# A row vector kept in two adjacent PSUM banks while a fused transformer kernel runs its front, with six banks in rotation

## The chip, the cores and the metric

One NeuronCore of a Trainium2 chip runs the whole program in one launch. The metric is device time in microseconds (us). Of the kernel before there are three runs, with a median of 1686.18 us (1681.76 to 1689.4), and one execution under the profiler.

## The reference, cut to what matters

The reference is a small model on one sequence of 256 tokens with a width of 1024, in fp32. Every block of its first part is modulated by a vector that comes from a condition `c`:

```python
def modulation(cs, w, b):
    m = cs @ w + b                      # cs: 1 x 1024, w: 1024 x 3072
    shift, scale, gate = jnp.split(m, 3, axis=-1)
    return shift[:, None, :], scale[:, None, :], gate[:, None, :]

cs = jax.nn.silu(c)
for i in range(DEPTH):                  # DEPTH = 2
    shift, scale, gate = modulation(cs, mod_mix_w[i], mod_mix_b[i])
    h = x * (1.0 + scale) + shift
    y = mla_mixer(h, ...) if i == 0 else s5_mixer(h, ...)
    x = layer_norm(ALPHA * x + (1.0 + gate) * y, ln_mix_g[i], ln_mix_b[i])
    shift, scale, gate = modulation(cs, mod_ffn_w[i], mod_ffn_b[i])
    h = x * (1.0 + scale) + shift
    y = sq_relu_mlp(h, mlp_w1[i], mlp_b1[i], mlp_w2[i], mlp_b2[i])
    x = layer_norm(ALPHA * x + (1.0 + gate) * y, ln_ffn_g[i], ln_ffn_b[i])
```

A second part of two layers follows: gated MLPs before and after a mixer, which is a recurrent block with a convolution and a gated linear recurrence in the first layer, and block attention with a bias in the second.

## The kernel before

All weights are streamed from device memory once, in blocks of 128 rows of 1024 columns (512 KB), in the order in which they are needed; `run` takes the next blocks of that list. A block of a matrix (`w`) is split into two fp32r tiles: ScalarE makes `wh`, a rounded copy (L464), and VectorE makes `wl`, the rest (L504; for some blocks GpSimd, L468). A matrix product is then three matmuls (xh by wh, xh by wl, xl by wh) that add up in a PSUM bank (L400). The activations are split the same way by `split` (L636 on ScalarE, L637 on VectorE).

A block of the modulation weights (`m`, each holds 128 outputs with 1024 inputs) doesn't go to TensorE. `mod_unit` multiplies it on VectorE with `cs`, the row silu(c) repeated on all 128 partitions (128 x 1024), and adds up along the row in the same instruction (L555). There are 96 such products; 40 of them run in the first 110 us, which the text calls the front. After each group of eight, L564 adds the bias.

The program is written in Python that calls the engines in program order (a manual schedule); each engine works off its own queue in that order, and waits between engines are put in by the tile framework from the tiles that instructions read and write.

PSUM is divided into eight bank tiles of 128 x 512. `self.free` is a queue of bank numbers: `bank()` takes the number at its front, `rel()` puts a bank that has been read at its end. So which bank a step gets follows from the order of takes and releases alone.

The order of the work, as far as the change and the prediction touch it:
- `setup` makes constants, and `cs` out of two banks (L1013 on ScalarE, L1014 on VectorE).
- `mla`: input projections; GpSimd computes the tables of the S5 mixer beside them (the rotations, L1421). Then `q_pair(0)` and `heads`, the loop over eight attention heads, with three further `q_pair`. A `q_pair` makes the queries of two heads on TensorE; VectorE turns part of them (L1227, L1228, L1229), and their sum is the operand of the scores. After the loop the output projection `mla_o` starts.
- From there on, for each block: `boundary` runs the last pass of a projection, the norm of its result, the transposes of the normed rows (L644, four into each of two banks), and `make_xt`, which applies scale and shift while it moves two banks to SBUF, one on ScalarE (L679), the other on VectorE (L677), in four pieces each; `xt_split` splits the result. Then `f_pass(0)` and `f_pass(1)` compute four hidden tiles for the two halves of the tokens into two banks each, and `f_evac` moves these out, one bank on ScalarE (L901), the other on VectorE (L902).

The pieces of `make_xt` are issued like this:

```python
for j in range(4):
    for g in range(2):
        if g:
            nc.vector.tensor_scalar(o, i, s[:, k:k + 1], sh[:, k:k + 1], op0=OP.mult, op1=OP.add)
        else:
            nc.scalar.activation(o, i, func=AF.Identity, scale=s[:, k:k + 1], bias=sh[:, k:k + 1])
```

Of the kernel before, what the change touches and what calls it, by code (L numbers as in the profile page):

```python
# [11 lines left out]
F32 = mybir.dt.float32  # L12
F32R = mybir.dt.float32r
I32 = mybir.dt.int32
AF = mybir.ActivationFunctionType
OP = mybir.AluOpType
# [296 lines left out]
class Model:  # L313
    def __init__(self, ctx, tc, ws, cols, rows, x, pos, inv, rel, sp, sbc, sgb, out):
        self.tc, self.nc = tc, tc.nc
        self.ws, self.rows_d, self.x_d, self.pos_d, self.inv_d = ws, rows, x, pos, inv
        self.cols_d, self.relb_d, self.sp_d, self.sbc_d, self.sgb_d, self.out_d = cols, rel, sp, sbc, sgb, out
        sb = self.sb = ctx.enter_context(tc.tile_pool(name="sb", bufs=1))
        ps = ctx.enter_context(tc.tile_pool(name="ps", bufs=1, space=bass.MemoryType.PSUM))
        dr = ctx.enter_context(tc.tile_pool(name="dr", bufs=1, space=bass.MemoryType.DRAM))  # L320
        T = lambda n, shape, dt=F32: sb.tile(shape, dt, name=n)
        self.raw = [T("raw%d" % i, [128, 1024]) for i in range(RAWN)]
        self.Hs, self.Ls = [None] * RING, [None] * RING
        self.pt = {u: sb.tile([128, 1024], F32, name="early%d" % j, tag="w%s%d" % ("hl"[j % 2], 4 + j // 2))
                   for j, u in enumerate(PUNITS)}
        self.lent = {4 + j: set(PUNITS[2 * j:2 * j + 2]) for j in range(5)}
        self.lent[9] = self.lent[10] = {"tables"}
        self.tabs = [[sb.tile([128, 1024], F32, name="rot%d%d" % (b, e), tag="w%s%d" % ("hl"[e], 9 + b)) for e in range(2)]
                     for b in range(2)]
        self.wide = [sb.tile([128, 2048], F32, name="wide%d" % i, tag="x%s" % "hl"[i]) for i in range(2)]  # L330
        self.rt, self.nop, self.opdone = [], 0, set()
        self.hidden(0)
        self.X = [T("x%d" % h, [128, 1024]) for h in range(2)]
        self.R = [T("r%d" % h, [128, 1024]) for h in range(2)]
        self.GATE, self.GR, self.BR, self.B2 = (T(n, [128, 1024]) for n in ("gate", "grow", "brow", "b2row"))
        self.Z = [T("z%d" % i, [128, 2048]) for i in range(3)]
        self.cols = T("cols", [128, NCOLS])
        self.ident = T("ident", [128, 128])
        self.mask = T("mask", [128, 128])
        self.identb, self.maskb = (T(n, [128, 128], mybir.dt.bfloat16) for n in ("identb", "maskb"))  # L340
        self.st = T("st", [128, 144])
        self.junk = T("junk", [128, 1024], mybir.dt.bfloat16)
        self.junka = T("junka", [128, 512], mybir.dt.bfloat16)
        self.mcol = [[T("mc%d%d" % (i, t), [128, 8]) for t in range(2)] for i in range(4)]
        self.scol, self.bcol = T("scol", [128, 8]), T("bcol", [128, 8])
        self.cs = T("cs", [128, 1024])
        self.msum, self.gcol = T("msum", [128, 8]), T("gcol", [128, 8])
        self.mhalf = T("mhalf", [128, 4])
        self.one = T("one", [128, 1])
        self.lri = T("lri", [128, 8], I32)  # L350
        self.banks = [ps.tile([128, 512], F32, name="bank%d" % i) for i in range(8)]
        self.free = deque(range(8))
        self.held = {}
        self.ops_d = dr.tile([12, 128, 1024], F32, name="ops_d")
        self.tab_d = dr.tile([4, 128, 1024], F32, name="tab_d")
        self.wt_d = dr.tile([2, 4, 2, 32, 64], F32, name="wt_d")
        self.stn = 0
        self.nproc = self.ntake = self.nw = 0
        self.pos_of, self.slot_owner = {}, [None] * RING
        self.slot_of, self.finished = {}, set()  # L360
        self.ndma = 0
        self.modfin, self.hold = None, False
        self.mods = set()
        self.pend = deque()
        self.lag, self.plo = False, deque()
        self.kept = {}
        self.xt32 = None
        self.bg = None
        self.bgt = 0.0
        self.fill = 0  # L370
# [8 lines left out]
    def bank(self):  # L379
        i = self.free.popleft()  # L380
        self.held[id(self.banks[i])] = i
        return self.banks[i]

    def rel(self, *bs):
        for b in bs:
            self.free.append(self.held.pop(id(b)))
# [158 lines left out]
    def mod_unit(self, u, raw):  # L545
        nc, tag, k = self.nc, u[1], u[2]
        i, third = int(tag[3]), int(tag[4])
        if k == 0 and third == 2:
            self.mod_finish()
        total = (self.gcol if tag == "mod01" else self.msum)[:, k:k + 1]  # L550
        if (tag, k) in POOLED:
            nc.gpsimd.tensor_tensor(raw, raw, self.cs, op=OP.mult)
            self.pend.append((raw, total))
        else:
            nc.vector.scalar_tensor_tensor(self.junk, raw, 1.0, self.cs, op0=OP.mult, op1=OP.mult, accum_out=total)  # L555
        if k == 7:
            self.settle(0)
        if tag == "mod01":
            if k == 7:
                self.mods.add(tag)  # L560
            return
        if k == 7:
            if third < 2:
                nc.vector.tensor_tensor(self.mcol[i][third], self.msum, self.col("modb%d" % i, 8 * third, 8), op=OP.add)  # L564
                self.mods.add(tag)
            else:
                nc.vector.tensor_tensor(self.gcol, self.msum, self.col("modb%d" % i, 16, 8), op=OP.add)
                nc.vector.tensor_scalar(self.gcol, self.gcol, 1.0, None, op0=OP.add)
                self.modfin = [tag, 3]
# [412 lines left out]
    def setup(self):  # L982
        nc = self.nc
        V, G = nc.vector, nc.gpsimd
        crow = self.GR[0:1, :]
        spt = self.wide[0][:, 768:768 + NSP]
        inv = self.wide[0][:, 864:896]
        posi = self.sb.tile([128, 2], I32, name="posi")
        nc.sync.dma_start(out=crow, in_=self.rows_d[ROWS["c"]:ROWS["c"] + 1, :])
        nc.sync.dma_start(out=spt, in_=self.sp_d)  # L990
        nc.sync.dma_start(out=posi, in_=self.pos_d)
        nc.sync.dma_start(out=inv, in_=self.inv_d)
        nc.sync.dma_start(out=self.cols, in_=self.cols_d)
        self._issue(2)
        for h in range(2):
            nc.sync.dma_start(out=self.X[h], in_=self.x_d[128 * h:128 * h + 128, :])
        self._issue(RAWN)
        half = self.Z[2][0:1, 0:128]
        V.memset(half, 0.5)
        V.memset(self.mhalf, -0.5)  # L1000
        V.memset(self.one, 1.0)
        jp = self.Z[0][:, 0:128]
        G.iota(jp, pattern=[[1, 128]], base=0, channel_multiplier=-1, allow_small_or_imprecise_dtypes=True)
        pi = self.sb.tile([128, 2], I32, name="pio")
        G.iota(pi[:, 0:1], pattern=[[0, 1]], base=0, channel_multiplier=1)
        V.tensor_scalar(self.ident, jp, 0.0, None, op0=OP.is_equal)
        V.tensor_scalar(self.mask, jp, 0.0, NEG, op0=OP.is_gt, op1=OP.mult)
        cb = [self.bank(), self.bank()]
        for n in range(2):
            self.mm(cb[n], half, crow[:, 512 * n:512 * n + 512], True, True)  # L1010
        for n in range(2):
            t = self.Z[0][:, 1024 + 512 * n:1536 + 512 * n]
            nc.scalar.activation(t, cb[n], func=AF.Tanh)  # L1013
            V.scalar_tensor_tensor(self.cs[:, 512 * n:512 * n + 512], t, 1.0, cb[n], op0=OP.add, op1=OP.mult)  # L1014
        self.rel(*cb)
        self.ssm_decay(spt, pi)
        posf = self.posf = self.stat(2)
        V.tensor_copy(posf, posi)
        self.inv = inv
# [90 lines left out]
    def mla(self):  # L1110
        nc = self.nc
# [7 lines left out]
        for k in range(8):  # L1119
            j = UNITS.index(("m", "mod01", k))  # L1120
            while self.nproc <= j:
                self.step()
            V.scalar_tensor_tensor(self.scol[:, k:k + 1], self.gcol[:, k:k + 1], 1.0, self.col("modb0", 8 + k),
                                   op0=OP.add, op1=OP.add)
# [112 lines left out]
        self.lag = True  # L1237
        self.heads(HEADS0, q_pair, qk, None, VV)
        self.lag = self.hold = False
        self.rests()  # L1240
        self.put_tables()
        self.need_mod("mod02")
# [868 lines left out]
```

## Time and profile before

| quantity | value |
|---|---|
| median of three runs | 1686.18 us (1681.76 to 1689.4) |
| the profiled execution, own time | 1684.43 us |
| its span from first to last instruction | 1682.7 us |
| mean granted clock of TensorE | 0.973 |
| busy share of PE, DVE, ACT, POOL | 94%, 67%, 50%, 14% |
| chain that ended last, by line | PE L400 48%, every other line 1% or less |

The span is shorter than the execution by what lies around it (1.7 us). In the rows below, PE is TensorE's matmuls, PEld its weight loads, DVE VectorE, ACT ScalarE, POOL GpSimd. A timeline row gives the start, the duration of the whole row, engine, line, operation, what it writes and reads, the shape, and how many instructions the row joins; at its end stands, if there was any, the idle time of the engine before it and whose result ended it. The granted clock is a share of TensorE's full clock. Names in the rows leave out numbers: all banks read "bank".

### The profile page before, as it was taken

What the parts mean: (1) busy time and instruction counts of PE and PEld (TensorE: products, weight loads), DVE (VectorE), ACT (ScalarE), POOL (GpSimd) and SP (SyncE); (2) the same over time, 40 slices, a digit from 0 to 9 for tenths busy, and PEclk for the clock granted to TensorE, in tenths of its full rate; (3) what the DMA queues carried; (4) which work ended last, traced back from release to release, by engine and by line L of the source; (5) the groups of instructions that cost most, each with busy time, mean ns of one, the idle gap of its engine ahead of it and who ended that gap; (6) DMA issues with size and microseconds to landing.
All of it is one profiled execution on the core that took longest, in us unless ns stands there. A gap on an engine that the chain in (4) does not pass through costs nothing.

```text
span 1682.7 us, 24904 instructions
## 1 busy us (share of the span) xinstructions
PE 1586.5 (94%) x9594; PEld 1398.7 (83%) x9594; DVE 1129.5 (67%) x1568; ACT 841.1 (50%) x1287; POOL 237.7 (14%) x309
## 2 busy tenths in 40 slices
PE   5879989998789999999999999999999999999998
PEld 2558888987778899789997779999899998779997
DVE  7877897779977755776554876555755555675553
ACT  3454567746355655354444855443644444664441
POOL 7990000013523000100000020000000001330000
PEclk9879999998889999999999999999999999999999
DMA  9774788968466565375551747564555653545540
GB/s 360 295 251 166 256 302 288 341 231 298 163 225 247 213 226 197 141 259 205 192 176 46 245 143 252 175 238 162 210 177 180 226 199 107 179 165 202 196 151 26
DMA packets 106586, 349.62 MB, mean 208 GB/s; under 512 B 12385, under 2 KB 22753, under 8 KB 106466
## 3 DMA queue, kind: packets, MB, share of 16 engines
q1 hardware_dynamic: 106466, 348.02, 59.1%
q8 instruction: 75, 1.23, 0.3%
q14 instruction: 45, 0.37, 0.1%
HBM read 338.41 MB, written 9.57 MB: 207 GB/s over the span
## 4 chain that ended last, share of the span: by engine, by line
PE 49%; DVE 4%; ACT 3%; issue 1%; POOL 1%; DMA 0%; DVEq 0%; POOLq 0%; ACTq 0%
PE bank L400 48%; ACT junka L693 1%; DVE wl L504 1%; PE bank L644 1%; ACT wh L464 0%; DMA raw<-in_ws_dram 0%; DVE r L731 0%; POOL wl L468 0%; DVE z L1844 0%; POOL st L689 0%; DVE z L1300 0%; DVE z L1910 0%; ACT r L1870 0%; DVE st L1284 0%; ACT z L1871 0%
## 5 line engine op out<-in xcount | busy, mean ns | idle before, releaser
L504 DVE TENSOR_TENSOR wl<-raw,wh 128x1024 fp32r<-128x1024 f32 x448 | 540.1, 1240 | 163.3 <-ACT wh L464 157.7
L464 ACT ACTIVATE wh<-raw 128x1024 fp32r<-128x1024 f32 x464 | 471.5, 1051 | 246.1 <-PE bank L400 141.9
L400 PE MATMUL bank<-xh,wh 128*128 128x256 f32 x1664 | 469.1, 282 | 0.0
L400 PE MATMUL bank<-xh,wl 128*128 128x256 f32 x1664 | 468.3, 281 | 0.0
L400 PE MATMUL bank<-xl,wh 128*128 128x256 f32 x1664 | 468.1, 281 | 0.0
L400 PEld LDWEIGHTS bank<-xh,wh 128*128 128x128 f32 x1664 | 317.0, 190 | 2.7 <-DVE z L1651 0.2
L400 PEld LDWEIGHTS bank<-xl,wh 128*128 128x128 f32 x1664 | 317.0, 190 | 2.1
L400 PEld LDWEIGHTS bank<-xh,wl 128*128 128x128 f32 x1664 | 316.9, 190 | 0.0
L400 PE MATMUL bank<-wh,hh 128*128 128x512 f32 x736 | 294.7, 400 | 4.3 <-ACT hh L636 4.3
L400 PE MATMUL bank<-wl,hh 128*128 128x512 f32 x736 | 291.4, 396 | 0.0
L400 PE MATMUL bank<-wh,hl 128*128 128x512 f32 x736 | 243.2, 396 | 7.9 <-DVE hl L637 4.3
L400 PEld LDWEIGHTS bank<-wh,hl 128*128 128x128 f32 x736 | 139.8, 190 | 40.8 <-DVE hl L637 4.9
L400 PEld LDWEIGHTS bank<-wh,hh 128*128 128x128 f32 x736 | 140.6, 191 | 35.1 <-ACT hh L636 5.9
L400 PEld LDWEIGHTS bank<-wl,hh 128*128 128x128 f32 x736 | 140.4, 191 | 28.5
L555 DVE SCALAR_TENSOR_TENSOR junk<-raw,cs 128x1024 bf16<-128x1024 f32 x96 | 129.3, 1347 | 4.2 <-DMA raw<-in_ws_dram 2.9
L689 POOL TENSOR_TENSOR st<-st,mhalf 128x1 f32<-128x1 f32 (+1 forms) x33 | 22.9, 693 | 747.5 <-DVE st L697 678.9
L400 PE MATMUL bank<-wl,xh 128*128 128x512 f32 x320 | 125.9, 393 | 2.2 <-DVE wl L504 1.3
L400 PE MATMUL bank<-wh,xh 128*128 128x512 f32 x320 | 126.2, 395 | 0.7 <-ACT wh L464 0.7
L637 DVE TENSOR_TENSOR hl<-z,hh 128x512 fp32r<-128x512 f32 x68 | 47.0, 692 | 95.9 <-ACT hh L636 95.9
L400 PE MATMUL bank<-wh,xl 128*128 128x512 f32 x320 | 100.8, 392 | 2.0 <-DVE xl L637 2.0
L636 ACT ACTIVATE hh<-z 128x512 fp32r<-128x512 f32 x68 | 43.0, 633 | 104.4 <-DVE z L929 103.3
L468 POOL TENSOR_TENSOR wl<-raw,wh 128x256 fp32r<-128x256 f32 x64 | 60.7, 980 | 127.7 <-ACT wh L464 127.5
(380 smaller groups left out, 1683.3 us busy)
## 6 DMA issues: line engine op xcount, KB each, us to landing
raw<-in_ws_dram SPq DMA_DIRECT2D x580, 512.0 KB
early<-in_ws_dram SPq DMA_DIRECT2D x10, 512.0 KB
grow<-in_rows_dram SPq DMA_DIRECT2D x9, 512.0 KB
brow<-in_rows_dram SPq DMA_DIRECT2D x6, 512.0 KB
ophh<-ops_d SPq DMA_DIRECT2D x6, 512.0 KB
ophl<-ops_d SPq DMA_DIRECT2D x6, 512.0 KB
gate<-in_rows_dram SPq DMA_DIRECT2D x5, 512.0 KB
tab_d<-rot SPq DMA_DIRECT2D x4, 512.0 KB
```

The costliest lines, as they stand in the source:

```text
L400: self.nc.tensor.matmul(out, l, r, start=start, stop=stop)
L464: self.nc.scalar.activation(self.Hs[s], raw, func=AF.Copy)
L468: self.nc.gpsimd.tensor_tensor(self.Ls[s][:, w], raw[:, w], self.f32(self.Hs[s])[:, w], op=OP.subtract)
L504: self.nc.vector.tensor_tensor(self.Ls[s], raw, self.f32(self.Hs[s]), op=OP.subtract)
L555: nc.vector.scalar_tensor_tensor(self.junk, raw, 1.0, self.cs, op0=OP.mult, op1=OP.mult, accum_out=total)
L636: self.nc.scalar.activation(hdst, src, func=AF.Copy)
L637: self.nc.vector.tensor_tensor(ldst, src, self.f32(hdst), op=OP.subtract)
L644: self.nc.tensor.transpose(b[:, 128 * j:128 * j + 128], src[:, 128 * k:128 * k + 128], self.ident)
L689: self.nc.gpsimd.tensor_tensor(r, v, self.mhalf[:, 0:n], op=OP.pow)
L693: self.nc.scalar.activation(self.junka[:, 0:512], src, func=AF.Square, scale=scale, accum_out=s[:, n:n + 1])
```

## The change

Six banks stay single tiles. Banks 6 and 7 become the two halves of one tile `pair` of 128 x 1024. After `setup` has made `cs`, `keep_row` takes both halves out of the rotation and ScalarE copies `cs` into `pair`. As long as it stands there, the products of `mod_unit` that run on VectorE read `pair` in place of `cs`. After `heads`, `drop_row` appends 6 and 7 to the queue of free banks, and the products read `cs` in SBUF again.

```diff
-        self.banks = [ps.tile([128, 512], F32, name="bank%d" % i) for i in range(8)]
+        self.banks = [ps.tile([128, 512], F32, name="bank%d" % i) for i in range(6)]
+        self.pair = ps.tile([128, 1024], F32, name="pair")
+        self.banks += [self.pair[:, 0:512], self.pair[:, 512:1024]]
+        self.csrow = None
...
+    def keep_row(self):
+        if self.csrow is None and 6 in self.free and 7 in self.free:
+            self.free.remove(6)
+            self.free.remove(7)
+            self.csrow = self.pair
+            self.nc.scalar.activation(self.pair, self.cs, func=AF.Copy)
+
+    def drop_row(self):
+        if self.csrow is not None:
+            self.csrow = None
+            self.free.extend((6, 7))
...
-            nc.vector.scalar_tensor_tensor(self.junk, raw, 1.0, self.cs, op0=OP.mult, op1=OP.mult, accum_out=total)
+            nc.vector.scalar_tensor_tensor(self.junk, raw, 1.0, self.cs if self.csrow is None else self.csrow, op0=OP.mult,
+                                           op1=OP.mult, accum_out=total)
...
         self.rel(*cb)
+        self.keep_row()
         self.ssm_decay(spt, pi)
...
         self.heads(HEADS0, q_pair, qk, None, VV)
         self.lag = self.hold = False
+        self.drop_row()
```

The lines of the changed program are shifted by 16 to 19 (L400 is L416, L555 is L571, L644 is L661, L677 and L679 are L694 and L696, L902 is L919). No engine's instructions change their order. What changes is the bank that each step gets and, with it, the waits. Three places show it. A name with a number behind it is a tile; `[waits X]` names the engines that the instruction waits for, and `x3` joins like rows.

The first place is ScalarE and VectorE in `make_xt` ahead of the S5 mixer's input projection, second half of the tokens (`z_98` takes the scaled rows, `xh` is the split operand). ScalarE before:

```order
L679 ACTIVATE z_98<-bank_126,bcol,scol 128x32x4 [waits PE_49]
L679 ACTIVATE z_98<-bank_126,bcol,scol 128x32x4 x3
L636 ACTIVATE xh<-z_98 128x4x128 [waits Activation_49]
L636 ACTIVATE xh<-z_98 128x4x128 [waits DVE_49]
L1591 ACTIVATE oph_2842<-ophh,spp 128x8x64 [waits DMAHW6_49]
```

ScalarE with the change:

```order
L696 ACTIVATE z_98<-pair,bcol,scol 128x32x4 [waits PE_49]
L696 ACTIVATE z_98<-pair,bcol,scol 128x32x4 [waits DVE_49] x3
L653 ACTIVATE xh<-z_98 128x4x128 [waits Activation_49]
L653 ACTIVATE xh<-z_98 128x4x128 [waits DVE_49]
L1610 ACTIVATE oph_2842<-ophh,spp 128x8x64 [waits DMAHW6_49]
```

VectorE's four pieces there read `z_98<-bank_123` before, with one wait for PE ahead of the four; now they read `z_98<-pair`, with a wait for ScalarE ahead of each. Nothing has moved; each of the three later pieces on ScalarE now waits for VectorE.

The second place is TensorE at the start of `f_pass(1)` of the first MLP (`wh8`, `wl8` are a weight block, `xh`, `xl` the activations; a row is one matmul into the bank named first). Before:

```order
L400 MATMUL bank5_128<-wh4_49_708,xl_929 128x512
L400 MATMUL bank3_126<-wh4_49_708,xl_929 128x512
L400 MATMUL bank0_123<-wh8_58_814,xh_928 128x512 [waits Activation_49]
L400 MATMUL bank0_123<-wl8_58_815,xh_928 128x512
L400 MATMUL bank4_127<-wh8_58_814,xh_928 128x512
```

With the change:

```order
L416 MATMUL bank0_123<-wh4_49_708,xl_929 128x512
L416 MATMUL pair_129<-wh4_49_708,xl_929 128x512
L416 MATMUL pair_129<-wh8_58_814,xh_928 128x512 [waits DVE_49,Activation_49]
L416 MATMUL pair_129<-wl8_58_815,xh_928 128x512
L416 MATMUL bank4_127<-wh8_58_814,xh_928 128x512
```

The first pass now ends in one half of `pair`, and the second starts in the other half; the first matmul there has gained a wait for VectorE, which moves the first half out.

The third place is TensorE in the last MLP passes ahead of the second part's first block (`hh1`, `hl1` are hidden tiles, `r0` the normed rows whose transposes `make_xt` then reads). With the change:

```order
L416 MATMUL pair_129<-wh7_57_804,hl1_3657 128x512
L661 MATMUL pair_129<-ident_100,r0_90 128x128 [waits DVE_49]
L661 MATMUL pair_129<-ident_100,r0_90 128x128 x3
L661 MATMUL bank4_127<-ident_100,r0_90 128x128 [waits DVE_49]
L661 MATMUL bank4_127<-ident_100,r0_90 128x128 x3
L416 MATMUL bank3_126<-wh8_58_814,hh1_3656 128x512
L416 MATMUL bank3_126<-wl8_58_815,hh1_3656 128x512
L416 MATMUL pair_129<-wh8_58_814,hh1_3656 128x512
```

Before, the first four transposes write `bank3_126`, the next four `bank4_127`, and neither accumulator of the passes is in these. Now the first transposes and the second accumulator are the two halves of `pair`.

## Rows read from the trace of the kernel before

**Rows 1.** The page: busy tenths of PE in 40 slices of 42 us.
```profile
PE   5879989998789999999999999999999999999998
```

**Rows 2.** Stretches: busy us of PE, PEld, DVE, ACT, POOL; clock, DMA share, GB/s.
```profile
50.00:60.00 10.00, 9.71 (x36) 6.55 (x34) 9.79 (x12) 5.01 (x10) 9.69 (x7) 0.95 1.03 407
```

**Rows 3.** Three lines of VectorE, first 130 us: duration ns min/median/max, first and last start.
```profile
L555 DVE SCALAR_TENSOR_TENSOR junk<-raw,cs x40: 1210/1278/2165, 9.3 to 109.0; 128x1024 bf16<-128x1024 f32 x40
...
L1227 DVE TENSOR_TENSOR z<-bank,brow x4: 413/425/425, 60.6 to 97.0; 128x256 f32<-128x256 f32 x4
...
L1229 DVE TENSOR_TENSOR z<-z x4: 425/454/640, 61.4 to 97.7; 128x256 f32<-128x256 f32 x4
```

**Rows 4.** Timeline of VectorE, 46 to 61 us.
```profile
46.22 1.22 DVE L555 SCALAR_TENSOR_TENSOR junk<-raw,cs 128x1024 bf16<-128x1024 f32 x1
...
47.48 1.52 DVE L555 SCALAR_TENSOR_TENSOR junk<-raw,cs 128x1024 bf16<-128x1024 f32 x1
...
55.49 0.89 DVE L564 TENSOR_TENSOR mc<-msum,cols 128x8 f32<-128x8 f32 x1
...
60.58 0.41 DVE L1227 TENSOR_TENSOR z<-bank,brow 128x256 f32<-128x256 f32 x1
```

**Rows 5.** Timeline of PE: last matmuls of the first q_pair, first scores after it.
```profile
56.74 2.54 PE L400 MATMUL bank<-gate,early 128*128 128x256 f32 x11
...
61.89 0.48 PE L400 MATMUL bank<-brow,z 64*128 64x256 f32 x1 [2.19 <-DVE z L1229]
```

**Rows 6.** Timeline of VectorE in the heads, 83 to 86 us.
```profile
83.49 1.75 DVE L555 SCALAR_TENSOR_TENSOR junk<-raw,cs 128x1024 bf16<-128x1024 f32 x1
...
85.28 0.88 DVE L564 TENSOR_TENSOR mc<-msum,cols 128x8 f32<-128x8 f32 x1
```

**Rows 7.** The page's group of L464, and VectorE at the end of setup.
```profile
L464 ACT ACTIVATE wh<-raw 128x1024 fp32r<-128x1024 f32 x464 | 471.5, 1051 | 246.1 <-PE bank L400 141.9
...
6.93 0.69 DVE L1014 SCALAR_TENSOR_TENSOR cs<-z,bank 128x512 f32<-128x512 f32 x1 [1.02 <-ACT z L1013]
...
9.26 1.22 DVE L555 SCALAR_TENSOR_TENSOR junk<-raw,cs 128x1024 bf16<-128x1024 f32 x1
```

**Rows 8.** Groups by form of VectorE: busy us, mean ns, then idle before.
```profile
L928 DVE SCALAR_TENSOR_TENSOR z<-z,bank 128x512 f32<-128x512 f32 x36 | 24.7, 687 | 44.0 <-ACT z L927 44.0
...
L1736 DVE SCALAR_TENSOR_TENSOR z<-z,z 128x512 f32<-128x512 f32 x4 | 2.8, 688 | 1.4 <-ACT z L1735 1.4
```

**Rows 9.** Timeline where the first MLP's second pass starts, PE and VectorE.
```profile
157.43 0.40 PE L400 MATMUL bank<-wh,xh 128*128 128x512 f32 x1
...
157.83 0.69 DVE L902 COPY z<-bank 128x512 f32<-128x512 f32 x1
```

**Rows 10.** Timeline of make_xt ahead of the S5 mixer, second half: three engines.
```profile
375.60 1.64 ACT L679 ACTIVATE z<-bank,bcol,scol 128x128 f32<-128x128 f32 x4 [7.60 <-PE bank L644]
...
376.04 1.48 DVE L677 TENSOR_SCALAR z<-bank,scol,bcol 128x128 f32<-128x128 f32 x4 [0.68 <-PE bank L644]
...
377.93 1.29 DVE L637 TENSOR_TENSOR xl<-z,xh 128x512 fp32r<-128x512 f32 x2 [0.41 <-ACT xh L636]
...
378.63 0.39 PE L400 MATMUL bank<-wh,xh 128*128 128x512 f32 x1
```

**Rows 11.** Timeline at the start of the second part, ScalarE and PE.
```profile
508.20 1.51 ACT L679 ACTIVATE z<-bank,bcol,scol 128x128 f32<-128x128 f32 x4 [2.15 <-PE bank L644]
...
509.75 1.38 ACT L636 ACTIVATE xh<-z 128x512 fp32r<-128x512 f32 x2
...
512.52 0.62 PE L400 MATMUL bank<-wh,hl 128*128 128x512 f32 x2
...
512.98 0.39 PE L400 MATMUL bank<-wh,xh 128*128 128x512 f32 x1
```

**Rows 12.** A late wait of PE, and the stretch behind it (columns as in rows 2).
```profile
698.55 1.61 PE L644 MATMUL bank<-ident,r 128*128 128x128 f32 x8 [3.05 <-DVE r L731]
...
698.50:702.00 3.50, 3.44 (x13) 2.82 (x14) 2.52 (x4) 2.14 (x3) 0.00 (x0) 0.63 0.00 0
```

## The prediction

> **What bounds the kernel now.** I read the slices of the page first. The PE line [rows 1] has 5, 8, 7 in its first three slices of 42 us and nearly only nines behind them: up to about 126 us something else sets the pace, and from there on TensorE does, so that in the long tail whatever holds PE up is paid in full, unless PE has to wait a little later anyway. The stretch table shows what the front is short of: between 50 and 60 us [rows 2] VectorE is busy 9.79 of 10 us, GpSimd 9.69, and the DMA queues stand at 1.03. Three resources are full at once; which of them ends a wait has to be looked up place by place.
>
> Then the source view of the line that the change edits [rows 3]. The 40 modulation products of the front take 1.210 us at best, 1.278 in the median, and 2.165 at worst. Two other lines in the same group tell why they vary: L1227, which has one operand in a bank, takes 0.413 to 0.425 whenever it runs; L1229, as wide, with both operands in SBUF, takes 0.425 to 0.640. GpSimd works its rotations all that time. So in this trace an operation of two SBUF operands is slowed beside GpSimd and one with a bank operand isn't. That is what the change can take away.
>
> **Part 1, the products.** Eight of them run from 46.22 to 60.58 us with one other operation in between, at 55.49 [rows 4]. The first has a pitch of 47.48 - 46.22 = 1.26, so eight would need 10.1; they took 60.58 - 46.22 = 14.36, less about 0.9 for the operation between, 13.4. So 3.3 us are lost. They can't all come back: L1227 at 60.58 needs the q_pair matmuls, and these end on PE at 56.74 + 2.54 = 59.28 [rows 5]. L1227 can move to 59.3, a gain of **1.3**. PE stood idle 2.19 us before its matmul of 61.89 on that chain [rows 5], so all 1.3 reach it.
>
> In the heads the product of 83.49 takes 1.75 [rows 6] where 1.21 is the best: 0.5, and behind it a chain of VectorE operations leads to the softmax. The small operation of 85.28 with 0.88 [rows 6] keeps two SBUF operands, and is left as it is. For the other products of the heads, of which most lie beside matmuls that PE has still to do, I take 1.2 (between nothing and 2.7, if each ran at 1.21 and stood on the path). The 18 products before 46 us I count at nothing: the queues are full there (1.03 in the row of 50 to 60), and a product that is done earlier waits for its weight block. If that cover were gone, their excess would be worth under 2 us. Front: -1.3 - 0.5 - 1.2 = **-3.0**, from -1 to -5.
>
> What does a bank operand itself cost? No row has 1024 columns out of two banks. Of 512 columns with a bank operand L928 takes 687 ns, and with two SBUF operands L1736 takes 688 [rows 8]. Equal, so I take 1.21; the upper bound is two of the 512 form, 1.37, by which the eight products above would only win back 3.3 - 8 x 0.16 = 2.0, and the front as a whole about 2. [...]
>
> **Part 2, the copy.** One ScalarE instruction is added, cs into the pair. L464 of the same size takes 1.051 us on average [rows 7]. cs is ready at 6.93 + 0.69 = 7.62, the first product starts at 9.26 [rows 7], and ScalarE has nothing to do in between: hidden, 0. If it came late by a hand-over, the first product would slip 0.3, and it would be caught up in the stretch that waits for DMA.
>
> **Part 3, six banks in the front.** In the listing no instruction is moved, so a bank that is missing shows only as a wait for a release. The heads take two banks at a time and give them back within a head; I found no place where a seventh is asked for with the six still out. Cost 0, at most 0.5.
>
> **Part 4, the pair as banks 6 and 7 afterwards.** This is where I think the time goes the other way. The two halves are one tile, and the listing shows that the program puts waits between users of different halves: three places stand in the rows of the change.
> - At 157.43 PE starts the next pass of the first MLP [rows 9]. Its bank is now one half, and VectorE's copy of 157.83 reads the other until 158.52. PE waits: **+1.1**.
> - At 375.60 ScalarE and, from 376.04, VectorE evict four pieces each [rows 10], at the same time. They are through at 376.04 + 1.48 = 377.52, after 1.92 us. Now each waits for the other's piece: 1.64 + 1.48 = 3.12, so +1.2 without any hand-over, and eight hand-overs. The trace shows 0.41 us of idle time between ScalarE's conversion and VectorE's next operation [rows 10]; bounded by 0 and 0.41 each I take 0.2, in all 1.2 + 1.6 = **+2.8** (1.2 to 4.5). PE wants the result at 378.63 [rows 10] with no slack.
> - At 508.20 ScalarE starts such an eviction while PE goes on with the MLP's last passes, whose second accumulator is the other half. It must wait for the last matmul of these, in the row of 512.52, at about 513.0 [rows 11]. From its start to the first converted half it was 509.75 + 0.69 - 508.20 = 2.24; PE's next pass, started at 512.98, comes at 515.2 to 515.4: **+2.3**.
> - Four smaller meetings of a PE write with a VectorE read of the other half come later. A read of a bank takes 0.69 (L928, rows 8); each meeting costs from nothing to two such reads, 0.7 on the average: **+2.8** (0 to 5.5).
>
> Sum +9.0. Some of it vanishes where PE waits anyway for something that isn't late: at 698.55 PE had been idle 3.05 us for VectorE [rows 12]. I take off **3.0** (0 to 3.05). Net of part 4: **+6.0**.
>
> **Sum.** -3.0 + 6.0 = +3.0. The profiled execution took 1684.43, so 1687.4; the median of the three runs lies 1.75 above it, which makes **1689.2 us**, say 1689. My forecast is no change: a measurement of this kernel can tell about 0.5% from none, 8.4 us.
>
> **The rivals.**
> (a) *The waits aren't there.* ScalarE and VectorE read two banks at once in the trace of before (375.60 and 376.04, rows 10), so nothing on the chip stands against it; only the program's waits do, and much of what they cost may be slack. Then the front's gain stays: 1686.2 - 3.0 = 1683, with the upper bound of the front 1681. Against it: the waits stand in the listing, and PE has no slack at 378.63. [...] Chance 0.15, of which 0.04 reaches below -0.5%.
> (b) *Slower: the clock falls in the new stalls.* After PE's idle 3.05 us at 698.55 the granted clock of 698.5 to 702 is 0.63 [rows 12], that is, for a part of it the lower of the two levels; 0.37 x 3.5 = 1.3 us there and more in the next stretch, 1.3 to 2.4 in all. New stalls of 2.8 and 2.3 us lie just under the idle time of that row; if they come to 3 us, two drops cost up to 4.8. That gives 1689.2 + 4.8 = 1694.0. With nothing taken off at 698 either, 1697; with the dearer product too, 1698. The deciding point is the idle time of PE at 378 and 513: near 3 us, or 2. Chance 0.17, of which 0.12 lies above +0.5%.
> (c) *The change doesn't do what it says:* products in the front stay slow beside GpSimd, because the other operand and the output are still in SBUF, or they take 1.37 to 1.4 for two banks. Then 1689.2 + 2 to 3 = 1692. Against it: L1227 and L1229. Chance 0.13, of which 0.01 above +0.5%.
> The forecast has what is left, 0.55.
>
> **How the numbers follow.** Faster by over 0.5% (under 1677.8): 0.04. Slower by over 0.5% (over 1694.6): 0.13. Between: 0.83. The range of 8 in 10 takes in (a) with the front's upper bound, 1681, and ends between the two prices of (b), at 1697: 1681 to 1697.
>
> **What would show it right or wrong.** In the profile of the changed kernel: line L571's products in the front at 1.21 to 1.30 with no value near 2 us (part 1; values near 1.4 everywhere speak for (c)). L1227's counterpart about a microsecond earlier than 60.58, and the first matmul of the output projection some 3 us earlier than before. The copy between 7.6 and 9.3. At about 375 the pieces of ScalarE and VectorE taking turns, and PE idle for 2 to 3 us behind them; ScalarE's eviction of 508 beginning only when PE's pass ends. The granted clock behind these two stalls decides between the forecast and (b). I'm wrong if the front gives more than 5 us, if PE's idle time after the front grows by under 3 or by over 12 us, or if some bank that is missing in the heads makes PE wait there.

## The result, and the profile after

| kernel | runs | median us | ratio to before, 95% interval |
|---|---|---|---|
| before | 7 | 1686.18 | |
| with the change | 7 | 1697.36 (1691.08 to 1699.55) | 1.0061 [1.0043, 1.0078] |

The change is slower by 0.6%: some 10 us by the ratio, 11.2 between the medians. The profiled execution took 1697.52 us, near the median; the one of before, with 1684.43, is 1.75 under its own, so these two lie 13.1 apart. Everything below asks where +10 came from when the front was to give something back.

The front did. These are the lines of the page and the source view that answer to [rows 3]:

```profile
PE 1588.3 (94%) x9594; PEld 1398.0 (82%) x9594; DVE 1120.7 (66%) x1568; ACT 843.8 (50%) x1288; POOL 202.8 (12%) x309
```

```profile
L571 DVE SCALAR_TENSOR_TENSOR junk<-raw,pair x40: 1203/1220/1222, 9.1 to 105.5; 128x1024 bf16<-128x1024 f32 x40
```

All 40 products now take 1.20 to 1.22 us, where 1.210 was the best before; the 2.17 is gone, and 1024 columns out of two banks cost nothing that shows. GpSimd's busy time went down as well, though no instruction of it was touched; one group of its rotations, in the group view, before and then after (busy us, mean ns):

```profile
L1421 POOL TENSOR_TENSOR wide<-rot,spp 128x512 f32<-128x512 f32 x8 | 12.8, 1621 | 0.3
```

```profile
L1440 POOL TENSOR_TENSOR wide<-rot,spp 128x512 f32<-128x512 f32 x8 | 9.1, 1155 | 0.3
```

So the slowing was mutual: with one operand in PSUM the products are free of it, and GpSimd's busy time falls from 237.7 us to 202.8. In e3 (below), which differs from the change in that operand alone, GpSimd is back at 236.7 us, and so is this group:

```profile
L1439 POOL TENSOR_TENSOR wide<-rot,spp 128x512 f32<-128x512 f32 x8 | 12.8, 1620 | 0.3
```

The timeline of the change shows the copy, the end of the eight products, and the two places in the heads ([rows 4] to [rows 7] answer to it):

```profile
7.47 1.03 ACT L393 ACTIVATE pair<-cs 128x1024 f32<-128x1024 f32 x1 [0.76 <-DVE cs L1031]
...
9.07 1.22 DVE L571 SCALAR_TENSOR_TENSOR junk<-raw,pair 128x1024 bf16<-128x1024 f32 x1
...
54.10 0.57 DVE L581 TENSOR_TENSOR mc<-msum,cols 128x8 f32<-128x8 f32 x1
...
55.97 1.22 DVE L571 SCALAR_TENSOR_TENSOR junk<-raw,pair 128x1024 bf16<-128x1024 f32 x1
...
59.51 0.42 DVE L1245 TENSOR_TENSOR z<-bank,brow 128x256 f32<-128x256 f32 x1 [2.31 <-PE bank L416]
...
60.78 0.70 PE L416 MATMUL bank<-brow,z 64*128 64x256 f32 x2 [0.95 <-DVE z L1247]
...
83.69 0.17 DVE L581 TENSOR_TENSOR mc<-msum,cols 128x8 f32<-128x8 f32 x1
```

The copy fits in its gap. VectorE is through with the eight products 2.3 us before q_pair is, and waits for PE; the scores start at 60.78, 1.1 earlier than in [rows 5]. The small operation that took 0.88 in [rows 6] takes 0.17 here, where GpSimd has its wide rotations behind it (the last ends at 78.4); beside them, at 54.10, it takes 0.57 in place of the 0.89 of [rows 4].

The front as a whole is read from the first matmul of the output projection, in the timelines of before, of the change and of e1 (below):

```profile
121.79 0.77 PE L400 MATMUL bank<-wh,hh 128*128 128x512 f32 x1
```

```profile
118.25 0.77 PE L416 MATMUL bank<-wh,hh 128*128 128x512 f32 x1
```

```profile
117.13 0.71 PE L421 MATMUL bank<-wh,hh 128*128 128x512 f32 x1
```

It comes 3.5 us earlier in the change and 4.7 in e1; in e3, without the operand in PSUM, it starts at 121.80, as before.

Behind the front, TensorE's waits tell the rest. The table of its waits (waiter, what it waited for: us in total, times, longest) has these lines of the new tile, among others, and before has no wait for these steps:

```profile
PE pair L416 <- DVE z L1784: 11.3, 1, 11.3
...
PE pair L416 <- ACT grow L1897: 3.4, 1, 3.4
...
PE pair L416 <- DVE r L758: 2.0, 1, 2.0
...
PE pair L416 <- DVE r L916: 1.5, 1, 1.5
...
PE pair L416 <- DVE z L919: 1.1, 1, 1.1
```

One correction to the part ahead of the prediction: its third place (508 us) is the output projection of the S5 mixer ahead of the second MLP, not the end of an MLP ahead of the second part. Times, tiles and waits are as given there.

### The profile page after: what moved, and what is told of

It reads as the page before. It is cut to its first block, busy times and chain, and to the rows that moved or that the text cites. A ratio compares the mean times of both kernels' runs of the same rounds, so it can differ in the third digit from the quotient of the medians.

```text
span 1695.7 us, 24912 instructions
## 1 busy us (share of the span) xinstructions
PE 1588.3 (94%) x9594; PEld 1398.0 (82%) x9594; DVE 1120.7 (66%) x1568; ACT 843.8 (50%) x1288; POOL 202.8 (12%) x309
## 4 chain that ended last, share of the span: by engine, by line
PE 50%; DVE 4%; ACT 3%; issue 1%; POOL 0%; DMA 0%; DVEq 0%; POOLq 0%; ACTq 0%
PE bank L416 37%; PE pair L416 12%; DVE wl L520 1%; ACT junka L710 1%; PE bank L661 0%; DMA raw<-in_ws_dram 0%; POOL wl L484 0%; DVE z L1863 0%; DVE z L1319 0%; ACT wh L480 0%; DVE wl L552 0%; DVE st L1303 0%; DVE xl L654 0%; POOL st L706 0%; DVE r L748 0%
## 5 line engine op out<-in xcount | busy, mean ns | idle before, releaser
L416 PE MATMUL bank<-xh,wh 128*128 128x256 f32 x1408 | 397.1, 282 | 0.0
L416 PE MATMUL bank<-xh,wl 128*128 128x256 f32 x1408 | 396.4, 282 | 0.0
L416 PE MATMUL bank<-xl,wh 128*128 128x256 f32 x1408 | 396.2, 281 | 0.0
L416 PEld LDWEIGHTS bank<-xh,wh 128*128 128x128 f32 x1408 | 268.1, 190 | 2.3 <-issue 0.2
L416 PEld LDWEIGHTS bank<-xl,wh 128*128 128x128 f32 x1408 | 268.2, 190 | 1.9
L416 PEld LDWEIGHTS bank<-xh,wl 128*128 128x128 f32 x1408 | 268.2, 191 | 0.0
L416 PE MATMUL bank<-wh,hh 128*128 128x512 f32 x466 | 185.9, 399 | 1.9 <-ACT hh L653 1.9
L416 PE MATMUL bank<-wl,hh 128*128 128x512 f32 x466 | 183.7, 394 | 0.0
L416 PE MATMUL bank<-wh,hl 128*128 128x512 f32 x466 | 166.5, 394 | 2.5 <-DVE hl L1940 2.5
L416 PE MATMUL pair<-wh,hh 128*128 128x512 f32 x270 | 107.7, 399 | 3.3 <-DVE r L758 2.0
L416 PE MATMUL bank<-wh,xh 128*128 128x512 f32 x256 | 102.9, 402 | 4.9 <-ACT xh L653 4.3
L416 PEld LDWEIGHTS bank<-wh,hl 128*128 128x128 f32 x466 | 88.0, 189 | 23.5 <-DVE hl L1940 3.4
L416 PE MATMUL pair<-wh,hl 128*128 128x512 f32 x270 | 102.4, 395 | 5.1 <-DVE hl L654 5.1
L416 PE MATMUL pair<-wl,hh 128*128 128x512 f32 x270 | 106.8, 396 | 0.0
L416 PEld LDWEIGHTS bank<-wh,hh 128*128 128x128 f32 x466 | 88.5, 190 | 21.1 <-ACT hh L653 3.1
L416 PE MATMUL bank<-wl,xh 128*128 128x512 f32 x256 | 102.0, 398 | 2.2 <-DVE wl L520 1.3
L416 PEld LDWEIGHTS bank<-wl,hh 128*128 128x128 f32 x466 | 88.4, 190 | 17.4
```

The lines of the kernel that those rows point to most:

```text
L416: self.nc.tensor.matmul(out, l, r, start=start, stop=stop)
```

## The experiments

Two theories stood against each other. **A**: the loss comes from waits between users of the two halves of one tile. **B**: it comes from the order in which banks go around after the front, which the change permutes. A third, **C**, blamed the front itself (six banks, the copy).

### e1: the same order of banks, but two tiles

```diff
+        self.ctx, self.pctx = ctx, ExitStack()
+        p2 = self.pctx.enter_context(tc.tile_pool(name="ps2", bufs=1, space=bass.MemoryType.PSUM))
+        self.pair = p2.tile([128, 1024], F32, name="pair")
+        self.banks += [None, None]
...
             self.csrow = None
+            self.pctx.close()
+            p3 = self.ctx.enter_context(self.tc.tile_pool(name="ps3", bufs=1, space=bass.MemoryType.PSUM))
+            self.banks[6:8] = [p3.tile([128, 512], F32, name="bank%d" % i) for i in (6, 7)]
             self.free.extend((6, 7))
```

> The row stands in a tile of two banks until the end of the heads, as in the change; then that tile is given up and two single bank tiles take its place as banks 6 and 7. Bank numbers and their order are those of the change. Theory A (the loss comes from waits between the two halves of one tile, +16 us behind the front; the front gives -3.4, as the first matmul of the output projection shows): 1686.2 - 3.4 = 1683, between 1681 and 1685, and TensorE's 11.3, 3.4, 2.0 and 1.5 us waits on the pair are gone. Theory B (the loss comes from the permuted order in which banks go around after the front): the order is unchanged, so 1697, between 1694 and 1700. Theory C (it comes from the front: six banks, or the copy): 1697 as well.

Measured: 1679.65 us, ratio 0.9960 [0.9943, 0.9977]. A holds, B and C fall: with the bank order, the copy and the six banks of the change kept, the loss turns into a gain of 0.4%. The four waits are gone: e1's table has no line of the pair. The gain is more than the 3.4 us that were expected; 1683 is outside the runs' range (1675.54 to 1682.63). The eviction ahead of the S5 mixer, in the timeline of e1, runs on both engines at once again, out of the two banks that are the pair in the change, as in [rows 10]:

```profile
370.72 1.64 ACT L701 ACTIVATE z<-bank,bcol,scol 128x128 f32<-128x128 f32 x4 [7.60 <-PE bank L666]
...
371.15 1.47 DVE L699 TENSOR_SCALAR z<-bank,scol,bcol 128x128 f32<-128x128 f32 x4 [0.68 <-PE bank L666]
```

### e2: the order alone, eight single tiles, no row

```diff
-        self.banks = [ps.tile([128, 512], F32, name="bank%d" % i) for i in range(6)]
-        self.pair = ps.tile([128, 1024], F32, name="pair")
-        self.banks += [self.pair[:, 0:512], self.pair[:, 512:1024]]
+        self.banks = [ps.tile([128, 512], F32, name="bank%d" % i) for i in range(8)]
...
-            self.csrow = self.pair
-            self.nc.scalar.activation(self.pair, self.cs, func=AF.Copy)
+            self.csrow = True
...
-            ... self.cs if self.csrow is None else self.csrow ...
+            ... self.cs ...
```

> Eight single bank tiles; banks 6 and 7 leave the rotation at the end of setup and come back after the heads as in the change, but no row is kept: the products read cs in SBUF. Theory A: the time of before, 1686, between 1684 and 1688. Theory B: the loss of the change without its gain in the front, 1697 + 3 = 1700. Theory C (six banks in the front cost the time): near 1697 to 1700, with TensorE late by 10 us at 157 us already.

Measured: 1688.64 us, ratio 1.0006 [0.9992, 1.0020]: no change that can be told. Six banks in the front and the new order cost at most 3.4 us. B is out a second time, and C with it. One thing doesn't fit well: in e2's profiled execution TensorE stands 4.7 us behind before at 157 us (C had named 10). In e3, with the same six banks and the same order, it stands with before there, so the six banks alone don't make it; why e2 has it is open.

### e3: the change with its row unused

```diff
-            ... self.cs if self.csrow is None else self.csrow ...
+            ... self.cs ...
```

> The change with its copy and its pair of banks, but the products of the front read cs in SBUF. Only the gain in the front is taken out. Theory A: 1697.4 + 3.4 = 1700.8, between 1698.5 and 1703; the products in the front spread from 1.2 to 2.1 us again. If the front's gain came from something else than the operand in PSUM: 1697, as the change.

Measured: 1701.03 us, ratio 1.0097 [1.0073, 1.0121], as A had it. Taking the operand out of PSUM brings the spread of the products back, in the source view of e3:

```profile
L571 DVE SCALAR_TENSOR_TENSOR junk<-raw,cs x40: 1209/1278/2167, 9.0 to 109.0; 128x1024 bf16<-128x1024 f32 x40
```

### e4 and e5: the shared tile in one half of the program

e4 swaps the pair for two tiles at the start of the second MLP (about 514 us); e5 does the reverse, starting from e1. The swap stands in `rel`, which acts as soon as both banks are free; e4's:

```diff
+        if self.want and 6 in self.free and 7 in self.free:
+            self.want = False
+            self.pctx.close()
+            p3 = self.ctx.enter_context(self.tc.tile_pool(name="ps3", bufs=1, space=bass.MemoryType.PSUM))
+            self.banks[6:8] = [p3.tile([128, 512], F32, name="bank%d" % i) for i in (6, 7)]
...
         st = self.ssm(st)
+        self.want = True
```

> The change up to the start of the second MLP (about 514 us); from there the pair is given up for two single bank tiles, in the same order. Theory A, by TensorE's lateness against before in the trace of the change (+3.2 us at 514, +13.0 at the end): 1686.2 + 3.2 = 1689.4, between 1687 and 1691, the lower end if a later wait of TensorE absorbs a part. Theory B: 1697. A third view, that the waits before 455 us (of which the 11.3 us one is the longest) carry the loss: 1694 or more.

> The mirror of e4: two single tiles from the end of the heads to the start of the second MLP, the shared pair from there to the end; the bank order is that of the change throughout. Theory A, by the lateness of the change against e1 (+8.4 us of +18.5 at 509 us): e1's 1679.7 and the remaining 10.1 = 1689.8, between 1687 and 1692, with TensorE waiting about 3.4 us for ScalarE near 935 us and no wait of 11 us near 415. If the two halves of the loss aren't independent (a late TensorE absorbs what comes later): below 1687 or above 1693.

Measured: e4 1685.19 us, ratio 1.0006 [0.9993, 1.0019]; e5 1684.04 us, ratio 0.9991 [0.9978, 1.0003]. Against e1 the first part costs 0.46% (7.8 us), the second 0.31% (5.2 us); between the medians it is 5.5 and 4.4. Both parts are in it; neither alone carries the loss, and the view that the waits before 455 us carry it (1694 or more for e4) is out. Both came out below what I expected (1689.4 and 1689.8): e4's expectation took the front's gain as 3.4, and e5's read the second part off a single pair of profiled executions. e5 also lies below 1687, which I had named as the sign that the two parts aren't independent. By the ratios they add up to 13 us where the change loses 17 to e1; with intervals of 3 to 4 us on each, it stays open whether the rest is chance or whether the parts feed each other.

### e6: other meetings

```diff
-            self.free.extend((6, 7))
+            self.free.extendleft((7, 6))
```

> The change, with one edit: after the heads the two halves are put at the front of the queue of free banks in place of its end. Row, copy, six banks and the shared tile are as in the change; only which steps meet on the two halves differs. Theory A says that the loss belongs to those meetings: the waits of 11.3 us at 420 and 3.4 us at 938 should go or move, and the time should differ from 1697 by 3 us or more, either way, but stay over e1's 1680 by at least 4. A theory by which a bank that belongs to a tile of two is slower as such: 1697 again, within 2.

### e7: nothing but the shared tile

In the kernel before:

```diff
-        self.banks = [ps.tile([128, 512], F32, name="bank%d" % i) for i in range(8)]
+        self.banks = [ps.tile([128, 512], F32, name="bank%d" % i) for i in range(6)]
+        self.pair = ps.tile([128, 1024], F32, name="pair")
+        self.banks += [self.pair[:, 0:512], self.pair[:, 512:1024]]
```

> The kernel before with one edit: banks 6 and 7 are the halves of one tile from the first instruction on. No row, no copy, eight banks in rotation, bank order of before, products from SBUF. Theory A: slower than before by some 5 to 20 us (the change loses 17 to e1 by its meetings; these are others, and there are more of them, as the front takes part), so 1691 to 1706. Theory B (order): the order is that of before, so 1686, between 1684 and 1688.

Measured: e6 1722.14 us, ratio 1.0208 [1.0191, 1.0225]; e7 1728.57 us, ratio 1.0245 [1.0228, 1.0263]. One tile in place of two, with everything else as before, costs 41 us, twice the upper end of what I had expected; and moving the two numbers to the other end of the queue makes the change 25 us slower. e7 keeps the order of before, so its loss is the shared tile's. e6 also permutes the order, and that order with single tiles wasn't run, so its 25 us aren't shown to be the tile's alone; but the theory of a bank that is slower as such (1697 again) is out. The waits have moved to other steps (e6 has neither the 11.3 nor the 3.4 of the change), as the wait tables of e6 and then of e7 show:

```profile
PE pair L416 <- ACT z L1754: 14.7, 1, 14.7
PE pair L416 <- ACT z L954: 9.5, 3, 3.2
PE pair L416 <- ACT grow L1471: 9.1, 2, 6.0
```

```profile
PE pair L402 <- ACT z L939: 16.1, 4, 6.0
PE pair L402 <- DVE r L1653: 8.1, 1, 8.1
PE pair L402 <- DVE st L1286: 7.1, 2, 5.2
```

The change as it was made had drawn a mild order. Not all of e7's loss is idle time: the same 9594 matmuls keep TensorE busy for 1608.9 us against 1586.5 of before, at a mean granted clock of 0.959 against 0.973, so about half of the loss (an estimate from these busy times) goes with the lower clock.

## Why the prediction was right and wrong, step by step

The forecast was no change at 1689 us. The ratio puts the change at 1696.5 (1.0061 x 1686.18), just inside the range that ended at 1697; its median, 1697.36, is just outside. It is slower by over 0.5%, which had a chance of 0.13. The front came out as forecast; the loss behind it was seen, but at a third of its size. To place the loss I compare the starts of the same matmul in the profiled executions of e1 and of the change:

| place | change late behind it, us | added there | in the sum |
|---|---|---|---|
| front | about 1.1 | (the same program up to there) | |
| 157, first MLP, second pass | 2.5 | 1.4 | 1.1 |
| 378, make_xt ahead of the S5 mixer | 4.9 (2.7 ahead) | 2.2 | 2.8 |
| 420, in the S5 mixer | 16.4 | 11.5 | not there |
| 455 | 5.1 | -11.3 | not there |
| 513, make_xt ahead of the second MLP | 8.8 (4.8 ahead) | 4.0 (wait 2.4, clock 1.5) | 2.3 |
| 698, late wait | 8.9 | 0.1 | -3.0 |
| 938 to 941, recurrent block | 15.6 | 6.7 | not there |
| 962 to 968 | 11.7 | -3.9 | not there |
| the four smaller meetings | 17.3 (12.3 ahead) | 5.0 | 2.8 |
| 1489, no wait of the pair | 18.5 | 1.2 (clock) | not there |
| end | 18.0 | | |

(The places are named by before's times; small steps in between are left out. It is one execution against one: e5, the same program as e1 up to 514 us, runs some 3 us ahead of it by 486.)

**Part 1, the products: right.** I took 3.0; by the first matmul of the output projection it is 3.5 in the change and 4.7 in e1. (e1's ratio, 6.7 us with an interval of 3.9 to 9.6, is of the whole program.) The 1.3 at the first scores was 1.1 in the change and 2.0 in e1. One term was put at nothing and wasn't nothing: the two-operand operations beside the products, "left as it is". The one of 85.28 went from 0.88 to 0.17, as GpSimd, no longer held up by the products, is through with its rotations earlier (at 78.4, before at 95.5).

**The bank operand, the copy, six banks: right.** 1.203 to 1.222 us where 1.21 was taken; the upper bound of 1.37 is not in the rows. The copy is hidden. e2 bounds six banks together with the new order.

**Part 4, three places: right.** Without the clock they come to 6.0 in place of 6.2. At 378 the timeline of the change shows the turns of the two engines, and PE's wait behind them:

```profile
373.91 0.59 ACT L696 ACTIVATE z<-pair,bcol,scol 128x128 f32<-128x128 f32 x1 [8.04 <-PE pair L661]
...
374.53 0.51 DVE L694 TENSOR_SCALAR z<-pair,scol,bcol 128x128 f32<-128x128 f32 x1 [1.30 <-ACT z L696]
...
375.08 0.58 ACT L696 ACTIVATE z<-pair,bcol,scol 128x128 f32<-128x128 f32 x1 [0.58 <-DVE z L694]
...
375.70 0.51 DVE L694 TENSOR_SCALAR z<-pair,scol,bcol 128x128 f32<-128x128 f32 x1 [0.65 <-ACT z L696]
...
377.97 1.17 ACT L653 ACTIVATE xh<-z 128x512 fp32r<-128x512 f32 x2
...
378.66 0.50 PE L416 MATMUL bank<-wh,xh 128*128 128x512 f32 x1 [2.00 <-ACT xh L653]
```

One of the engines always stands still for the other's piece. The piece that starts at 373.91 ends at 374.50, and VectorE starts at 374.53; a hand-over costs 0.03 to 0.04, not the 0.2 that I took. The pieces cost more: one by itself takes 0.49 to 0.59, where the four in a row of [rows 10] have a pitch of 0.41.

**Part 4, what I took off: wrong.** The 3.0 at 698 didn't come. The wait is as long as in [rows 12], in the timeline of the change:

```profile
702.39 1.78 PE L661 MATMUL bank<-ident,r 128*128 128x128 f32 x8 [3.06 <-DVE r L748]
```

VectorE's norm there needs TensorE's own last pass; TensorE late makes VectorE late (its operations of that norm are all 8.8 behind e1, like TensorE), and nothing is absorbed. The question to ask of such a wait is whether its releaser hangs on the waiter's earlier work. A wait of the other sort stood at 420:

```profile
431.49 0.69 PE L416 MATMUL pair<-ophl,z 128*64 128x128 f32 x2 [11.25 <-DVE z L1784]
```

11.25 us, the longest of all, and by 455 it is given back whole (e4, which has it too, is 1.3 behind e1 there): in this stage TensorE builds operators ahead of their use, and GpSimd sets the pace. In the timeline of e1 TensorE comes early to the same stage and waits there:

```profile
438.19 0.44 PE L421 MATMUL bank<-oph,z 128*64 128x128 f32 x2 [2.92 <-POOL z L1691]
440.97 0.48 PE L421 MATMUL bank<-opl,z 128*64 128x128 f32 x1 [2.34 <-POOL z L1695]
```

Between 434 and 454 us the change has no wait for GpSimd.

**Part 4, a place that I missed, and the clock.** At 938 (of before) the gates of the recurrent block fill both halves one after the other. The timeline of the change:

```profile
938.74 1.89 PE L416 MATMUL pair<-z,raw 128*128 128x256 f32 x8
940.47 1.89 PE L416 MATMUL bank<-z,raw 128*128 128x256 f32 x8
945.76 3.78 PE L416 MATMUL pair<-z,raw 128*128 128x256 f32 x8 [3.40 <-ACT grow L1897]
...
944.87 0.84 ACT L1897 ACTIVATE grow<-pair,cols 128x256 f32<-128x256 f32 x2
```

The matmuls of 945.76 write one half and wait until ScalarE, which had a queue of gates and a table load (1.28 us, at 943.57) ahead of it, has read the other. In e1 the 32 matmuls are one row without a wait:

```profile
929.84 7.07 PE L421 MATMUL bank<-z,raw 128*128 128x256 f32 x32
```

Eight matmuls take 3.78 instead of 1.89. The stretch table of the change (columns as in [rows 2]) shows why, and the same behind the stall of 513 and behind a wait of 1.97 us at 1500.67:

```profile
515.27 0.80 PE L416 MATMUL bank<-wh,xh 128*128 128x512 f32 x1 [2.26 <-ACT xh L653]
...
511.40:514.80 3.40, 1.61 (x8) 0.99 (x6) 0.00 (x0) 1.72 (x5) 3.40 (x6) 1.00 0.65 218
514.80:518.20 3.40, 2.93 (x7) 2.35 (x8) 2.88 (x5) 2.83 (x4) 1.65 (x3) 0.54 0.55 172
...
944.80:948.20 3.40, 2.44 (x6) 2.00 (x7) 3.23 (x7) 1.62 (x5) 0.00 (x0) 0.55 0.04 16
948.20:951.60 3.40, 3.40 (x10) 2.69 (x9) 2.60 (x4) 1.96 (x4) 0.00 (x0) 0.50 0.00 0
...
1500.20:1503.60 3.40, 2.93 (x9) 2.32 (x10) 3.40 (x6) 0.00 (x0) 3.40 (x5) 0.69 0.96 364
```

The granted clock fell to 0.50, from 1.00 ahead of it (938 to 944.8); behind the other two waits the stretches have 0.54 and 0.69, and windows of half a microsecond in them 0.50. That is rival (b)'s mechanism, at one of the two places that it named (513) and at two that it didn't have. It costs 1.5 us behind 513 (lateness 7.3 to 8.8), 3.1 at 938 and 1.2 at 1500 (1489 in the table). Two of the three don't come with their wait every time: e4 has the same wait ahead of the second MLP without a fall. The two rows of e4:

```profile
511.21 0.50 PE L423 MATMUL bank<-wh,xh 128*128 128x512 f32 x1 [2.26 <-ACT xh L660]
...
510.70:514.10 3.40, 2.89 (x12) 2.37 (x13) 2.84 (x5) 2.88 (x4) 1.63 (x3) 1.00 0.50 175
```

The wait of 1.97 us stands in e1 too, at 1483.71, with a granted clock of 1.00 behind it. And it isn't all a loss: at 962 to 968 the change gets 3.9 back. It waits 2.0 us there where e1 waits 3.5, and e1 has a fall of its own behind that, which the change has not (2.4 of the 3.9). The stretch table of e1:

```profile
960.20:963.60 3.40, 1.49 (x4) 1.21 (x5) 2.93 (x5) 2.12 (x4) 0.00 (x0) 0.58 0.75 278
963.60:967.00 3.40, 3.40 (x10) 2.63 (x9) 2.67 (x5) 1.45 (x3) 0.00 (x0) 0.50 0.48 164
```

**The four smaller meetings: right places, nearly twice the size.** Their waits in the timeline of the change:

```profile
989.86 0.50 PE L416 MATMUL pair<-wh,hh 128*128 128x512 f32 x1 [2.01 <-DVE r L758]
...
1253.74 0.50 PE L416 MATMUL pair<-wh,xh 128*128 128x512 f32 x1 [1.52 <-DVE r L916]
...
1430.82 0.50 PE L416 MATMUL pair<-wh,xh 128*128 128x512 f32 x1 [0.43 <-DVE xl L654]
...
1443.37 0.50 PE L416 MATMUL pair<-wh,xh 128*128 128x512 f32 x1 [0.32 <-DVE r L919]
```

Together 4.3 us of waits, 5.0 with what follows, where 2.8 was taken, within the bound of 5.5.

**In sum:** front -3.0 was -3.5, part 4 +6.0 was about +17 (16.9 behind the front between the profiled executions of e1 and of the change; 17.0 by the ratios, 1.0061 less 0.9960), so +3.0 became +10 by the ratio to before and +13.1 between the profiled executions. The step that failed is the net of part 4. The meetings on its list came to 11.0 in place of 9.0; the 3.0 taken off at 698 weren't absorbed, as their releaser hangs on TensorE's own earlier work; a place that wasn't on the list, 938 with what 962 gives back, added 2.8; and the falls of the clock at 513 and 1500, which the sum had at nothing, added 2.7. One sign of being wrong that the prediction named itself came as well: by the stretch tables TensorE's idle time behind 130 us grew from 61.2 to 75.0 us, by more than 12.

That the time still lies near the range is in part luck. (b) had 1697 for two falls of the clock and nothing taken off; of its two falls one came, the other (378) didn't, and its number was reached by meetings that it didn't have. Its deciding point, an idle time near 3 us or near 2, decides nothing here: 2.26 us had a fall in the change and none in e4.

**The rivals.** (a), that the program's waits cost nothing, is out; but its other half, that nothing on the chip needs them, is what e1 shows for these two banks: they are read by two engines at once (370.72 and 371.15 above) as soon as they are two tiles. (c), that the products stay slow, is out by the source views of the change and e3.

## What to carry to other kernels

A wait is put in for a tile, not for a bank: joining two banks in one tile makes users of the one wait for users of the other, in the listing of make_xt even where both engines only read, and here that alone cost 41 us (e7). If an operand has to span banks for one stage, give its tile a pool of its own, close it after the stage, and open single tiles in its place (e1: 0.9960, the best of the versions here). A VectorE operation with two SBUF operands beside a busy GpSimd is worth a look in the timeline: one operand in PSUM gave time back to both engines (the change against e3: products of 1203 to 1222 ns against 1209 to 2167, GpSimd busy for 202.8 us against 236.7).

## What the runs showed of the hardware that I had not expected

- The slowing beside GpSimd is mutual: GpSimd's 128x512 rotations went from 1621 to 1155 ns, and its busy time from 237.7 (of before) to 202.8 us; e3, without the operand in PSUM, has 1620 ns and 236.7 us.
- A product with 1024 fp32 columns out of two banks takes 1203 to 1222 ns; the best one with both operands in SBUF takes 1210.
- The length of one wait didn't decide whether the granted clock fell. In the change it fell behind waits of 2.26 us (0.54 at 514.8 to 518.2) and 1.97 us (0.69 at 1500.2 to 1503.6), and stayed at 1.00 behind the waits of 2.00 at 378.66 and 2.01 at 989.86. In e4 it stayed at 1.00 behind the 2.26 us at the same step. So a single profiled execution doesn't tell what such a wait costs.
